# A transformer layer's down projection: written order, and a fourth block by seven half products

## The chip, the core and the metric

The kernel runs on one core of one Trainium2 chip. The metric is the device time of one execution in microseconds (us), the median of repeated runs; lower is better. The engines that appear below are PE (the matrix engine, TensorE), DVE (VectorE, elementwise work on 128 partitions), ACT (ScalarE), POOL (GpSimd) and SP (SyncE, which here issues the transfers that bring the weights from memory). Each engine works through its own list of instructions in order, and waits on semaphores for the others.

## The reference, cut to what matters

One layer of a diffusion transformer on 256 tokens of width 2048, with a 256-token context prefix: adaLN modulation, one combined q/k/v projection, windowed and global attention, an output projection, a residual with LayerNorm, and then the feed-forward half, where the change is:

```python
def modulate(x, shift, scale):
    return x * (1.0 + scale) + shift

def swiglu(u, w_gate, w_up, w_down):
    return (jax.nn.silu(u @ w_gate) * (u @ w_up)) @ w_down

# x: (1, 256, 2048); w_gate, w_up: (2048, 5632); w_down: (5632, 2048); all float32
x = layer_norm(DN_ALPHA * x + g2 * swiglu(modulate(x, sh2, sc2), w_gate[layer], w_up[layer], w_down[layer]),
               ln2_g[layer], ln2_b[layer])
```

## The kernel before, in words

**A product.** Everything is float32, and PE multiplies in a rounded form of it. So each operand is split in two: `hi` is the rounded value (a cast on ACT) and `lo` what the rounding left (a subtraction on DVE). A product of a 128x128 piece of the left operand with a 128x512 piece of a weight is then three matmuls into one accumulation bank: hi by hi, hi by lo, lo by hi (`mm3`, L333 to L335). A weight piece of 512 rows and 512 columns is loaded whole (1 MB, SP's queue, L303) into one of four `raw` buffers, and split in two halves of 128x1024 elements each (L323 cast, L324 subtraction; `split`, L329 and L330, does the same to any operand). There are four `hi` and four `lo` buffers, taken in turn, so that the splits run at most four halves ahead of PE.

**The feed-forward half.** The hidden width of 5632 is cut into 11 blocks, f = 0 to 10, of 512. For each block the gate and up projections (`project`, in four groups g of input features) give two sums; then come the steps of its tail: `turned` (silu, product, squares), `puts` and `gets` (out to memory and back, which transposes), and `places`, which splits the result into `hTh` and `hTl`, the left operands of the down projection. A tail step doesn't stand where it is due in the code: it is put in a list with a count, and each projection call or each step of the down projection counts one (`turn`; a step by seven products counts two at its end). When the count is reached, the tail step's instructions are written down there. ACTIVATE 2, PUT 6, GET 8 and PLACE 9 are the counts.

**The down projection** makes 256 tokens (two tiles t of 128) by 2048 columns, in two pairs of column blocks of 512 (`pair(0)` and `pair(2)`). The sum over the 11 blocks f can be done in two ways. A plain step takes a block f and one column block: one load, two halves of splits, 24 matmuls. A step by seven products takes f and both column blocks of a pair: the 256x512 left operand and the 512x1024 weight are cut into quarters, and Strassen's method in Winograd's form gives the product of the two 2x2 arrangements with seven products of quarters in place of eight. Such a step has two loads, seven splits, 42 matmuls (a pair of plain steps has 48), and four additions or subtractions of weight quarters on DVE, 128x1024 elements each (`by_quarters`). The sums of left quarters that it needs are made once per block (`quarter_sums`, by `QUARTERS`: the count for `places` and that for the sums). The seven products go to three extra banks (p5, p6, p7), and to the banks of the ordinary sums; when all steps by seven products are done, `combine_parts` puts the extra banks into the second column block's sums. `first_block` and `second_block` then apply the gate row (L1245), add to the residual (L1246) and take statistics (L1249) for a column block that is done.

Before the change f = 8, 9 and 10 go by seven products, and a pair is done in the order `ORDER`: first all f for the first column block (with the steps by seven products among them), then the plain f for the second. The gate and up projections stand inside a region whose engines keep the written order. The down projection stands outside it: there a scheduler with costs of its own sets the order on each engine, and only the last column block's end on DVE and ACT is in written order. Of the second pair's last column block the last three plain steps are loaded and split together, and their matmuls are then done tile by tile of tokens, so that token tile 0 is complete while PE works on tile 1; `ending` normalises and stores each. One of the three is split into a `raw` buffer instead of the `hi` and `lo` ones (it is called `hilo` in the rows).

Of the kernel before, what the change touches and what calls it, by code (L numbers as in the profile page):

```python
# [23 lines left out]
P = 128  # L24
# [38 lines left out]
GATE_ROWS = ((17, 20, 23, 23, 24, 27), (43, 44, 47, 47, 48, 51))  # L63
# [195 lines left out]
def dit_layer(ctx: ExitStack, tc: tile.TileContext, x, c, cx, c_ctx, w_ada, b_ada, w_in, q_norm_g,  # L259
# [1266 lines left out]
    u2h = pb.tile([P, KD, SEQ], F32R, tag="u2h", name="u2h")  # L1526
    u2ls = [pb.tile([P, KD // 2, SEQ], F32R, tag=f"u2l{i}", name="u2l") for i in range(2)]

    def u2l(k, n=1):
        half = u2ls[k // (KD // 2)]  # L1530
        k %= KD // 2
        return half[:, k : k + n, :] if n > 1 else half[:, k, :]
# [3 lines left out]
    def z_part(kk):  # L1536
# [9 lines left out]
        nc.scalar.copy(u2h[:, kk : kk + 2, :], uf)  # L1546
        nc.vector.tensor_tensor(u2l(kk, 2), uf, u2h[:, kk : kk + 2, :].bitcast(F32), op=ALU.subtract)
# [11 lines left out]
    def project(accs, w_, f, g, first, last, seeded=False):  # L1559
        w = load_split(w_, g * 4, f * NB)  # L1560
        for j in range(4):
            k = g * 4 + j
            for t in range(NT):
                mm3(accs[t], u2h[:, k, t * P : (t + 1) * P], u2l(k)[:, t * P : (t + 1) * P], w[j],
                    k == first and not seeded, k == last, seeded)
# [27 lines left out]
    quarters, room = {}, {}  # L1593

    def quarter_sums(f, hf):
        i = list(QUARTERS).index(f)
        if i == 0:
            both = pb.tile([P, 2, 2, 4, 2, P], F32R, tag="u2h", name="quarters")
            room["q"] = [both[:, 0], both[:, 1], pb.tile([P, 2, 4, 2, P], F32R, tag="u2l0", name="quarters")]
            room["x"] = pb.tile([P, 2, 2 * NB], F32, tag="u2l1", name="sums")  # L1600
        quarters[f] = [room["q"][i][:, c] for c in range(2)]
        sums = room["x"][:, 0].rearrange("p (s q t) -> p s q t", s=4, q=2)
        s1, s2, s3, s4 = (sums[:, c].rearrange("p q (a i) -> p q a i", a=4) for c in range(4))
        (a11, a12), (a21, a22) = ([hf[t].rearrange("p (a q i) -> p q a i", a=4, q=Q)[:, k : k + 2] for k in (0, 2)]
                                  for t in range(NT))
        for o, x0, x1, op in ((s1, a21, a22, ALU.add), (s2, s1, a11, ALU.subtract), (s3, a11, a21, ALU.subtract),
                              (s4, a12, s2, ALU.subtract)):
            nc.vector.tensor_tensor(o, x0, x1, op=op)
        split(*quarters[f], sums)
# [65 lines left out]
    def z_rest(t, kk):  # L1675
# [7 lines left out]
        nc.scalar.copy(u2h[:, kk : kk + 2, tt], uf)  # L1683
# [121 lines left out]
    def plain(f, n, accs, begins, ends):  # L1805
        w = load_split(w_down, f * 4, n * NB)
        for t in range(NT):
            mms(f, w, t, accs[t], begins, ends)
# [160 lines left out]
```

## Time and profile before

| | |
|---|---|
| median of 3 runs | 1126.13 us (1125.84 to 1126.19) |
| the profiled execution | 1126.5 us, span from first to last instruction 1124.6 us |
| mean granted clock of PE | 0.996 |
| down projection, from the trace | from about 890 us of the span on; the last matmul starts at 1111.01 |

A row of a timeline gives the start in us, the duration, the engine, the line, the operation, what is written and read, and how many instructions the row holds; in square brackets the engine's idle time ahead of it and what ended that. A row of windows gives a stretch, its length, and for each of PE, its weight loads, DVE, ACT and POOL the busy time with the number of instructions that touch the stretch; then PE's granted clock, the busy share of the transfer engines, and GB/s. PE's matmuls overlap: a matmul that is shown with 0.39 us starts 0.23 us after the one ahead of it.

### The profile page before, as it was taken

Reading aid. Unit: us, or ns where it says so; the run is one execution under the profiler, and the core shown is the slowest. Engines: PE = TensorE matmul, PEld = TensorE weight load, DVE = VectorE, ACT = ScalarE, POOL = GpSimd, SP = SyncE. Lnnn points to the kernel's source line nnn. Section 1 sums busy time; section 2 is a strip of 40 time slices with the busy share of each in tenths; the row PEclk is TensorE's granted clock in tenths of the full one; section 3 lists DMA queues with packets and bytes.
Section 4 is the critical chain, followed back from the end, with each engine's and each line's share of the span. In section 5 each row is a group of like instructions: output and inputs, shape, how many; then the busy total and the mean of one; then the engine's idle time right before and its main releaser. Section 6 shows DMA issues by size and latency. Waiting matters only on the chain. (4 is left out here: it accounts for less than half of the span.)

```text
span 1124.6 us, 14148 instructions
## 1 busy us (share of the span) xinstructions
PE 1104.0 (98%) x5241; PEld 893.6 (79%) x5241; DVE 905.8 (81%) x1097; ACT 604.1 (54%) x879; POOL 39.8 (4%) x79
## 2 busy tenths in 40 slices
PE   8999999999999999999999999999999999999995
PEld 7677788788887787888888888888888788888884
DVE  3758999999998998778666876887875899678876
ACT  3335574887684355444564455655554565345541
POOL 1000040101200010000000000000000000000000
PEclk9999999999999999999999999999999999999998
DMA  9999999697999789989858798889896576546651
GB/s 299 388 389 382 386 362 371 227 313 209 358 318 378 267 317 326 341 304 341 287 197 290 266 349 284 302 310 306 302 318 219 169 251 215 194 143 243 226 204 75
DMA packets 179241, 321.26 MB, mean 286 GB/s; under 512 B 8762, under 2 KB 51162, under 8 KB 176867
## 3 DMA queue, kind: packets, MB, share of 16 engines
q1 hardware_dynamic: 177364, 319.25, 80.9%
q10 hardware_dynamic: 1808, 1.11, 0.3%
q8 instruction: 41, 0.67, 0.2%
q14 instruction: 28, 0.23, 0.1%
HBM read 304.07 MB, written 16.25 MB: 285 GB/s over the span
## 5 line engine op out<-in xcount | busy, mean ns | idle before, releaser
L324 DVE TENSOR_TENSOR lo<-raw,hi 128x1024 fp32r<-128x1024 f32 x234 | 282.8, 1221 | 129.0 <-ACT hi L323 126.8
L323 ACT CAST hi<-raw 128x1024 fp32r<-128x1024 f32 x234 | 245.4, 1055 | 247.3 <-PE acc L335 121.7
L334 PE MATMUL acc<-lo,u2h 128*128 128x512 f32 x448 | 175.0, 391 | 0.8 <-DVE lo L324 0.8
L335 PE MATMUL acc<-hi,u2l 128*128 128x512 f32 x448 | 174.6, 390 | 0.1
L333 PE MATMUL acc<-hi,u2h 128*128 128x512 f32 x448 | 174.3, 391 | 0.0
L601 ACT CAST hi<-raw 128x1024 fp32r<-128x1024 f32 (+1 forms) x86 | 87.4, 1030 | 90.5 <-PE acc L335 41.1
L452 DVE SCALAR_TENSOR_TENSOR adav<-raw,cs,adav 128x1024 f32<-128x1024 f32 (+1 forms) x96 | 114.3, 1191 | 6.1 <-DMA raw<-in_w_ada_dram 4.5
L604 DVE TENSOR_TENSOR lo<-raw,hi 128x1024 fp32r<-128x1024 f32 (+1 forms) x86 | 101.4, 1192 | 21.4 <-ACT hi L601 21.4
L333 PE MATMUL acc<-hi,hTh 128*128 128x512 f32 x272 | 105.8, 389 | 0.6 <-ACT hi L329 0.6
L334 PE MATMUL acc<-lo,hTh 128*128 128x512 f32 x272 | 105.8, 389 | 0.0
L335 PE MATMUL acc<-hi,hTl 128*128 128x512 f32 x272 | 105.7, 389 | 0.0
L333 PE MATMUL acc<-hi,uh 128*128 128x512 f32 x256 | 103.5, 404 | 0.1
L335 PE MATMUL acc<-hi,ul 128*128 128x512 f32 x256 | 100.2, 391 | 0.0
L334 PE MATMUL acc<-lo,uh 128*128 128x512 f32 x256 | 99.9, 390 | 0.0
L335 PE MATMUL wk<-hi,u2l 128*128 128x512 f32 x256 | 99.6, 389 | 0.0
L334 PE MATMUL wk<-lo,u2h 128*128 128x512 f32 x256 | 99.6, 389 | 0.0
L334 PEld LDWEIGHTS acc<-lo,u2h 128*128 128x128 f32 x448 | 84.1, 188 | 19.5 <-DVE lo L324 2.2
L333 PE MATMUL wk<-hi,u2h 128*128 128x512 f32 x256 | 99.6, 389 | 0.0
L333 PEld LDWEIGHTS acc<-hi,u2h 128*128 128x128 f32 x448 | 84.1, 188 | 18.7 <-ACT u2h L1683 1.1
L335 PEld LDWEIGHTS acc<-hi,u2l 128*128 128x128 f32 x448 | 84.1, 188 | 17.9 <-DVE u2l L1684 0.7
L333 PEld LDWEIGHTS acc<-hi,uh 128*128 128x128 f32 x256 | 48.2, 188 | 16.0 <-issue 4.6
L333 PEld LDWEIGHTS acc<-hi,hTh 128*128 128x128 f32 x272 | 51.1, 188 | 11.7 <-ACT hi L329 1.0
(287 smaller groups left out, 1742.2 us busy)
## 6 DMA issues: line engine op xcount, KB each, us to landing
raw<-in_w_ada_dram SPq DMA_DIRECT2D x63, 1024.0 KB
raw<-in_w_up_dram SPq DMA_DIRECT2D x44, 1024.0 KB
raw<-in_w_gate_dram SPq DMA_DIRECT2D x44, 1024.0 KB
raw<-in_w_down_dram SPq DMA_DIRECT2D x44, 1024.0 KB
raw<-in_w_ada_dram SPq DMA_DIRECT2D x66, 512.0 KB
raw<-in_w_in_dram SPq DMA_DIRECT2D x18, 1024.0 KB
raw<-in_w_out_dram SPq DMA_DIRECT2D x16, 1024.0 KB
pd<-hx SPq DMA_DIRECT2D x64, 128.0 KB
```

The costliest lines, as they stand in the source:

```text
L323: nc.scalar.copy(hi[:, :n], raw[:, s : s + n])
L324: nc.vector.tensor_tensor(lo[:, :n], raw[:, s : s + n], hi[:, :n].bitcast(F32), op=ALU.subtract)
L333: nc.tensor.matmul(ps, lhsT=xh, rhs=w[0], start=first, stop=False, skip_group_check=seeded)
L334: nc.tensor.matmul(ps, lhsT=xh, rhs=w[1], start=False, stop=False, skip_group_check=seeded)
L335: nc.tensor.matmul(ps, lhsT=xl, rhs=w[0], start=False, stop=last, skip_group_check=seeded)
L452: nc.vector.scalar_tensor_tensor(a[:, c : c + piece], raw[:, f : f + piece], cs[:, 4 * (g * (G4 * NB // w) + j) + 2, None], a[:, c : c + p ...
L601: nc.scalar.copy(hl.hi[:, :n], raw.t[:, s : s + n])
L604: nc.vector.tensor_tensor(hl.lo[:, :n], raw.t[:, s : s + n], hl.hi[:, :n].bitcast(F32), op=ALU.subtract)
```

## The change

Four things are altered together.

1. Block 7 goes by seven products too: four of eleven blocks. The orders of the two pairs are written out (`ORDERS`: `a` is a plain step for the first column block, `b` for the second, `s` a step by seven products).
2. `down()` as a whole stands in the region of written order, on all five engines.
3. The last block's (f = 10) gate and up calls go by feature groups: gate and up of group 0, then of group 1, and so on. The modulated input `u2h`, `u2l` is kept in four-group tiles, and the space of a group that both have read goes to the sums of left quarters, so that those of f = 7 and 8 are made beside block 10's calls, and those of f = 9 and 10 in the down projection's first steps.
4. In a step by seven products the order is b, p1, a, p7, p5, p6, c instead of p1, b, a, p7, p5, p6, c, and the combinations of weight quarters are made in place in the `raw` buffers rather than in two buffers of their own; three of the four stand behind p1's split. The sums of left quarters are split in two halves of 128x512 (with a buffer for two sums) instead of one piece of 128x1024. At the end `first_block` of the second pair is written behind the loads and splits of the last three steps.

```diff
-QUARTERS = {8: (9, 13), 9: (10, 11), 10: (9, 9)}
-ORDER = (0, 1, 8, 2, 3, 9, 4, 5, 6, 10, 7)
+QUARTERS = {7: (9, 13), 8: (10, 11), 9: (10, 9), 10: (9, 9)}
+ORDERS = ("a0 a1 a2 s7 a3 a4 s8 a5 a6 b0 s9 b1 b2 b3 s10 b4 b5 b6", "a0 a1 a2 s7 a3 a4 s8 a5 a6 s9 b0 b1 s10 b2 b3 b4 b5 b6")
...
     def quarter_sums(f, hf):
         i = list(QUARTERS).index(f)
-        sums = room["x"][:, 0].rearrange("p (s q t) -> p s q t", s=4, q=2)
...
-        for o, x0, x1, op in ((s1, a21, a22, ALU.add), (s2, s1, a11, ALU.subtract), (s3, a11, a21, ALU.subtract),
-                              (s4, a12, s2, ALU.subtract)):
-            nc.vector.tensor_tensor(o, x0, x1, op=op)
-        split(*quarters[f], sums)
+        hi, lo = quarters[f] = [pb.tile([P, 4, 2, P], F32R, tag=f"u2{c}{i}", name="quarters") for c in "hl"]
+        pair = pb.tile([P, 2, 2, P], F32, tag="qs", name="sums")
...
+        nc.vector.tensor_tensor(one, a21, a22, op=ALU.add)
+        nc.vector.tensor_tensor(two, one, a11, op=ALU.subtract)
+        split(hi[:, 0:2], lo[:, 0:2], pair)
+        nc.vector.tensor_tensor(one, a11, a21, op=ALU.subtract)
+        nc.vector.tensor_tensor(two, a12, two, op=ALU.subtract)
+        split(hi[:, 2:4], lo[:, 2:4], pair)
...
-    calls = [(f, i, g) for f in gus for i in range(2) for g in range(groups[f], ng)]
+    calls = [(f, i, g) for f in gus if f < SPLIT_F for i in range(2) for g in range(groups[f], ng)]
+    calls += [(f, i, g) for f in range(SPLIT_F, FFN // NB) for g in range(ng) for i in range(2)]
...
         for name, left, right, after in (
-            ("p1", "a11", b11, (x1, b22, b12, sub)),
-            ("b", "s4", b22, (b12, b12, b11, sub)),
-            ("a", "a12", b21, (x2, x1, b11, add)),
-            ("p7", "s3", x1, (b21, b21, x2, sub)),
+            ("b", "s4", b22, None),
+            ("p1", "a11", b11, ((b22, b22, b12, sub), (b12, b12, b11, sub), (b11, b22, b11, add))),
+            ("a", "a12", b21, None),
+            ("p7", "s3", b22, ((b21, b21, b11, sub),)),
             ("p5", "s1", b12, None),
-            ("p6", "s2", x2, None),
+            ("p6", "s2", b11, None),
             ("c", "a22", b21, None),
         ):
...
+    def down():
+        parts, combine_parts, first_block, second_block, _ = pair(0)
+        head, rest = parts("b6")
+        run(head)
+        combine_parts()
+        run(rest)
+        first_block()
+        parts, combine_parts, first_block, last_block, bank = pair(2)
+        head, mid, rest, end = parts("a2", "b1", "b4")
+        run(head)
+        second_block()
+        run(mid)
+        l2_loads()
+        run(rest)
+        combine_parts()
+        ws = [load_split(w_down, f * 4, 3 * NB, spare=f == 6) for f in (4, 5, 6)]
+        first_block()
         for t in range(NT):
-            gated(t, 3, two[5]("bd"[t]), t2k("yt"))
+            for f, w in zip((4, 5, 6), ws):
+                mms(f, w, t, bank("bd"[t]), False, f == 6)
+        for t in range(NT):
+            gated(t, 3, bank("bd"[t]), t2k("yt"))
             spread(t, 3)
             ending(t)
+
+    with tc.manual_schedule(engines={ET.DVE, ET.Activation, ET.PE, ET.Pool, ET.SP}):
+        down()
```

Three places on DVE show what the written order does. The first is the tail of block 10 (`hTl`, then the sums of its left quarters, `sums` and `quarters`) in pair 0, with the splits of the weights around it (`lo`). Before:

```order
L324 TENSOR_TENSOR lo_7927<-raw_7920,hi_7926 128x1024
L330 TENSOR_TENSOR hTl_7955<-hf_7918,hTh_7954 128x4x128
L1608 TENSOR_TENSOR sums_7614<-hf_7918 128x256
L1608 TENSOR_TENSOR sums_7614<-hf_7916,hf_7918 128x256
L1608 TENSOR_TENSOR sums_7614<-sums_7614,hf_7916 128x256
L324 TENSOR_TENSOR lo_7969<-raw_7966,hi_7968 128x1024
L1608 TENSOR_TENSOR sums_7614<-hf_7916,sums_7614 128x256
L324 TENSOR_TENSOR lo_7973<-raw_7966,hi_7972 128x1024
L330 TENSOR_TENSOR quarters_7613<-sums_7614,quarters_7613 128x1024
```

Now, behind the last split of s8 (`lo_7966`) and ahead of the first of a5 (`lo_7999`):

```order
L330 TENSOR_TENSOR lo_7966<-raw_7899,hi_7965 128x1024
L330 TENSOR_TENSOR hTl_7980<-hf_7975,hTh_7979 128x4x128
L330 TENSOR_TENSOR hTl_7980<-hf_7977,hTh_7979 128x4x128
L1604 TENSOR_TENSOR sums_7987<-hf_7977 128x256
L1605 TENSOR_TENSOR sums_7987<-sums_7987,hf_7975 128x256
L330 TENSOR_TENSOR quarters_7986<-sums_7987,quarters_7985 128x512
L1607 TENSOR_TENSOR sums_7987<-hf_7975,hf_7977 128x256
L1608 TENSOR_TENSOR sums_7987<-hf_7975,sums_7987 128x256
L330 TENSOR_TENSOR quarters_7986<-sums_7987,quarters_7985 128x512
L324 TENSOR_TENSOR lo_7999<-raw_7996,hi_7998 128x1024
L324 TENSOR_TENSOR lo_8003<-raw_7996,hi_8002 128x1024
```

Splits of weights stood among the tail's instructions before; now all of the tail stands in one piece ahead of the next split. On ACT the casts of block 10's tail likewise stand in one piece between the casts of s8 and a5.

The second place is a step by seven products in pair 2. Before:

```order
L1832 TENSOR_TENSOR sums_7614<-raw_8670,raw_8668 128x1024
L1832 TENSOR_TENSOR raw_8668<-raw_8668 128x2x512
L330 TENSOR_TENSOR lo_8673<-raw_8668,hi_8672 128x1024
L330 TENSOR_TENSOR lo_8684<-raw_8670,hi_8683 128x1024
L1832 TENSOR_TENSOR sums_7614<-sums_7614,raw_8668 128x1024
L330 TENSOR_TENSOR lo_8695<-raw_8670,hi_8694 128x1024
L1832 TENSOR_TENSOR raw_8670<-raw_8670,sums_7614 128x2x512
L330 TENSOR_TENSOR lo_8706<-sums_7614,hi_8705 128x1024
L330 TENSOR_TENSOR lo_8717<-raw_8668,hi_8716 128x1024
L330 TENSOR_TENSOR lo_8727<-sums_7614,hi_8726 128x1024
L330 TENSOR_TENSOR lo_8737<-raw_8670,hi_8736 128x1024
```

Now:

```order
L330 TENSOR_TENSOR lo_8747<-raw_8744,hi_8746 128x1024
L330 TENSOR_TENSOR lo_8757<-raw_8742,hi_8756 128x1024
L1827 TENSOR_TENSOR raw_8744<-raw_8744,raw_8742 128x2x512
L1827 TENSOR_TENSOR raw_8742<-raw_8742 128x2x512
L1827 TENSOR_TENSOR raw_8742<-raw_8744,raw_8742 128x2x512
L330 TENSOR_TENSOR lo_8770<-raw_8744,hi_8769 128x1024
L330 TENSOR_TENSOR lo_8780<-raw_8744,hi_8779 128x1024
L1827 TENSOR_TENSOR raw_8744<-raw_8744,raw_8742 128x2x512
L330 TENSOR_TENSOR lo_8791<-raw_8742,hi_8790 128x1024
L330 TENSOR_TENSOR lo_8801<-raw_8742,hi_8800 128x1024
L330 TENSOR_TENSOR lo_8811<-raw_8744,hi_8810 128x1024
```

The step has the same eleven instructions. The first load's buffer (`raw_8668` before, `raw_8742` now) was read for the last time by the fifth split, and now is by the sixth.

The third place is the end: the last splits (`lo`, `hilo`), `first_block` of pair 2 and the start of the last column block's end (`yt`). Before, `first_block`'s last rows (L1878 to L1249) stood ahead of the splits of the last five steps:

```order
L1878 TENSOR_TENSOR u_8996<-acc_8440,u_8996 128x512
L1245 TENSOR_TENSOR u_8996<-u_8996,adav_6163 128x512
L1246 TENSOR_TENSOR xt_76<-xt_76,u_8996 128x512
L1249 BN_STATS stats_77<-xt_76 128x6
L324 TENSOR_TENSOR lo_9090<-raw_9087,hi_9089 128x1024
...
L324 TENSOR_TENSOR hilo_9180<-raw_9175,hilo_9180 128x1024
L324 TENSOR_TENSOR lo_9168<-raw_9165,hi_9167 128x1024
L324 TENSOR_TENSOR lo_9172<-raw_9165,hi_9171 128x1024
L1245 TENSOR_TENSOR yt_9257<-acc_8538,adav_6163 128x512
```

Now:

```order
L324 TENSOR_TENSOR lo_9218<-raw_9211,hi_9217 128x1024
L324 TENSOR_TENSOR hilo_9223<-raw_9221,hilo_9223 128x1024
L324 TENSOR_TENSOR hilo_9226<-raw_9221,hilo_9226 128x1024
L1882 TENSOR_TENSOR c1_9189<-acc_8489,c1_9189 128x512
L1245 TENSOR_TENSOR c1_9189<-c1_9189,adav_6168 128x512
L1246 TENSOR_TENSOR xt_76<-xt_76,c1_9189 128x512
L1249 BN_STATS stats_77<-xt_76 128x6
L1882 TENSOR_TENSOR u_9190<-acc_8502,u_9190 128x512
L1245 TENSOR_TENSOR u_9190<-u_9190,adav_6168 128x512
L1246 TENSOR_TENSOR xt_76<-xt_76,u_9190 128x512
L1249 BN_STATS stats_77<-xt_76 128x6
L1245 TENSOR_TENSOR yt_9309<-acc_8599,adav_6168 128x512
```

`first_block` has moved behind the last splits, and the two `hilo` splits behind the last pair of `lo`.

More of the change, by code (lines that the diff above doesn't have):

```diff
@@ L1803, in mms @@
             mm3(ps, hTh[f][:, j, tt], hTl[f][:, j, tt], w[j], first and j == 0, last and j == 3)
[L1805 to L1808, printed above, removed]
-        turn()
     def by_quarters(f, n, bank, begins, ends):
@@ L1851, in begins, with step, plain_step @@
             return fresh
[L1853 to L1862 removed]
+        order = ORDERS[n // 2].split()
+        last = {k: [o for o in order if o[0] == k][-1] for k in "abs"}
+        steps = {}
+        def step(kind, f):
+            if kind == "s":
+                return lambda: by_quarters(f, n, bank, begins, f"s{f}" == last["s"])
+            ps, col = ("ac", n) if kind == "a" else ("bd", n + 1)
+            def plain_step():
+                w = load_split(w_down, f * 4, col * NB)
+                for t in range(NT):
+                    mms(f, w, t, bank(ps[t]), begins(ps[t]), f"{kind}{f}" == last[kind] and kind == "b")
+                turn()
+            return plain_step
+        for o in order:
+            steps[o] = step(o[0], int(o[1:]))
         def combine_parts():
```

95 lines of the change are left out of this document (30 added, 65 removed).

## The prediction

> **What bounds the kernel now.** I read the page's busy times first, then PE's waits in the down projection, then the windows and timelines around the places that the change touches.
>
> ```profile
> PE 1104.0 (98%) x5241; PEld 893.6 (79%) x5241; DVE 905.8 (81%) x1097; ACT 604.1 (54%) x879; POOL 39.8 (4%) x79
> PE acc L333 <- ACT hi L329: 0.6, 1, 0.6
> 1052.76 0.39 PE L333 MATMUL wk<-hi,hTh 128*128 128x512 f32 x1
> 1060.91 0.39 PE L333 MATMUL acc<-hi,hTh 128*128 128x512 f32 x1
> 1111.01 0.39 PE L335 MATMUL acc<-hilo,hTl 128*128 128x512 f32 x1
> ```
>
> PE is busy for 98% of the span, and from 870 us on it shows one wait, of 0.6 us: PE sets the pace of the down projection. What a matmul costs there is read from starts, not durations: a step by seven products begins its first product at 1052.76 and its seventh at 1060.91, with 36 matmuls between, so 8.15 / 36 = 0.226 us each. A product is then 1.36 us, a step by seven products (42) 9.52, a plain step (24) 5.44. Because rows of 0.39 us overlap, a PE that falls behind by a few tenths still looks busy; so a stall is found by counting matmuls:
>
> ```profile
> 890.00:895.00 5.00, 4.96 (x22) 3.78 (x21) 5.00 (x5) 2.77 (x3) 0.00 (x0) 1.00 0.41 113
> 895.00:900.00 5.00, 4.39 (x20) 3.31 (x19) 5.00 (x8) 3.87 (x4) 0.00 (x0) 1.00 0.46 140
> 900.00:905.00 5.00, 4.98 (x23) 3.78 (x22) 5.00 (x6) 3.52 (x6) 0.00 (x0) 1.00 0.94 341
> 905.00:910.00 5.00, 5.00 (x24) 4.14 (x23) 5.00 (x5) 1.87 (x2) 0.00 (x0) 1.00 0.97 346
> ```
>
> Here, where the down projection starts, DVE is busy in all of each 5 us and PE gets 22 + 20 + 23 = 65 matmuls through, against 72 at the rate of the row after: 7 x 0.226 = 1.6 us lost, partly to counting at the edges; I use 1.5. DVE is the second limit, and inside a step by seven products it is near:
>
> ```profile
> 1051.59 1.05 ACT L329 CAST hi<-raw 128x1024 fp32r<-128x1024 f32 x1 [3.02 <-PE acc L335]
> 1052.68 1.23 DVE L330 TENSOR_TENSOR lo<-raw,hi 128x1024 fp32r<-128x1024 f32 x1 [2.74 <-ACT hi L329]
> 1053.94 1.23 DVE L1832 TENSOR_TENSOR raw<-raw,sums 128x1024 f32<-128x1024 f32 x1
> 1055.08 1.22 DVE L330 TENSOR_TENSOR lo<-sums,hi 128x1024 fp32r<-128x1024 f32 x1
> 1056.21 1.22 DVE L330 TENSOR_TENSOR lo<-raw,hi 128x1024 fp32r<-128x1024 f32 x1
> 1057.35 1.22 DVE L330 TENSOR_TENSOR lo<-sums,hi 128x1024 fp32r<-128x1024 f32 x1
> 1058.48 1.22 DVE L330 TENSOR_TENSOR lo<-raw,hi 128x1024 fp32r<-128x1024 f32 x1
> ```
>
> The third product's cast waits 3.02 us for PE to give a buffer back, DVE's split follows, and then DVE runs through the addition, p7, p5, p6 and c without a gap, 1.135 us apart ((1058.48 - 1052.68) / 5 = 1.16 with the first). The step's last split ends at 1059.70, 6.94 after the step's first matmul; it is due at the seventh product, 8.15 after. So DVE is 1.2 us ahead at the end of such a step, and the next split is in time by about as much.
>
> **The change part by part.**
>
> *Fewer matmuls.* One more block by seven products saves 48 - 42 = 6 matmuls in each of two pairs: 12 x 0.226 = **-2.7 us**. Both ends of this are the same; a matmul here has no cheaper form.
>
> *Sums of left quarters beside block 10.* The stall at 890 to 905 is the tails of blocks 8 and 9 with their sums meeting the first splits of the down projection. Those of 7 and 8 now stand among block 10's calls, and those of 9 are taken apart. A plain or projection step needs two splits of DVE's 5.44 us, so about 3.2 us are free in each; the cover is there. I give back the whole stall, **-1.5** (bounds 0, if it only moves, and -1.6).
>
> *Block 10's tail between s8 and a5.* The tail's count of 9 falls on the end of s8 in pair 0, and in written order all of it stands between s8's last split and a5's first. Its pieces:
>
> ```profile
> 920.94 0.68 DVE L330 TENSOR_TENSOR hTl<-hf,hTh 128x512 fp32r<-128x512 f32 x1
> 921.54 0.75 DVE L1608 TENSOR_TENSOR sums<-hf 128x256 f32<-128x256 f32 x2
> 922.21 0.42 DVE L1608 TENSOR_TENSOR sums<-sums,hf 128x256 f32<-128x256 f32 x1
> 902.23 1.13 ACT L329 CAST hTh<-hf 128x512 fp32r<-128x512 f32 x2
> ```
>
> A subtraction of 128x512 takes 0.68 us (0.60 to the next start), a sum of 128x256 0.42, a cast of 128x512 1.13 / 2 = 0.57. Counted from s8's first matmul: the last split of s8 ends at about 7.3 (6.94 before; the three additions in a row ahead of the third product cost 0.3); two hTl to 8.4; two sums to 9.3; cast on ACT to 9.9; subtraction to 10.6; two sums to 11.4; cast to 12.0; subtraction to 12.7. The two sums have one buffer, so the second pair can't be made before the first cast and subtraction are through. ACT's cast for a5 stands behind the last tail cast and ends at 13.0; DVE's split for a5 runs from 13.0 to 14.2. PE needs that split for its second matmul of a5, at 9.52 + 0.23 = 9.75. What is late: 14.2 - 9.75 = **+4.5** (4.2 to 4.8 by this chain; 0 if tail and splits overlapped as before, where the scheduler put splits between the tail's instructions and PE showed no wait). DVE has nothing else to hide it: the ring of four halves lets no split of a5 pass the tail.
>
> *The end.* Before, the last splits, and what follows on DVE:
>
> ```profile
> 1094.84 2.58 DVE L324 TENSOR_TENSOR lo<-raw,hi 128x1024 fp32r<-128x1024 f32 x2 [0.51 <-ACT hi L323]
> 1103.28 0.69 DVE L1245 TENSOR_TENSOR yt<-acc,adav 128x512 f32<-128x512 f32 x1 [5.85 <-PE acc L335]
> 1104.00 0.69 DVE L1246 TENSOR_TENSOR xt<-xt,yt 128x512 f32<-128x512 f32 x1
> 1104.73 0.69 DVE L1249 BATCH_NORM_STATS2 stats<-xt 128x6 f32<-128x512 f32 x1
> 1112.06 0.68 DVE L1245 TENSOR_TENSOR yt<-acc,adav 128x512 f32<-128x512 f32 x1
> ```
>
> DVE was idle for 5.85 us ahead of token tile 0's end (the first yt), and from there to tile 1's yt it works 8.78 us without a gap, although tile 1's last matmul started at 1111.01: from 1103.28 on DVE sets the end. Now two things stand in that idle time: the two hilo splits, which have moved behind the last pair of ring splits (2 x 1.135 = 2.3 us), and the eight instructions of first_block (at the 0.72 us from one dependent 128x512 to the next, 1104.73 - 1104.00, 5.7 us). The last pair ends at 1097.42 as before, since it waits for buffers that PE frees; 1097.4 + 2.3 + 5.7 = 1105.4 against 1103.28: **+2.0** (1.5 to 2.4), and it goes to the end whole. Where first_block stood before, it and the splits had other slack; that gains nothing, since PE did not wait there.
>
> *first_block of pair 0* (written behind b6) and combine_parts (behind b5) put 16 such instructions, 11 us, around two splits of b6, ahead of pair 2's first split. By the same count from b5 this split is in time for a0's matmuls within a few tenths either way: **+0.4** (0 to 0.8).
>
> *The loads.* A step by seven products gives its two raw buffers back late, and the next such step takes them, if two plain steps lie between (two others use the other two buffers). That was so before between steps 8 and 9, and shows in pair 2:
>
> ```profile
> 1009.98 1.22 DVE L330 TENSOR_TENSOR lo<-raw,hi 128x1024 fp32r<-128x1024 f32 x1
> 1011.12 1.22 DVE L330 TENSOR_TENSOR lo<-sums,hi 128x1024 fp32r<-128x1024 f32 x1
> 1012.25 1.22 DVE L330 TENSOR_TENSOR lo<-raw,hi 128x1024 fp32r<-128x1024 f32 x1
> 1011.22 2.64 SPq L303 DMA_DIRECT2D raw<-in_w_down_dram  x2
> 1020.32 1.23 DVE L1832 TENSOR_TENSOR sums<-raw 128x1024 f32<-128x1024 f32 x1 [1.77 <-DMA raw<-in_w_down_dram]
> ```
>
> SP issues the first load when p5's split ends (1011.20) and the second when c's does (1013.47; its issue ends the 2.64 us). The second lands 6.8 us later, at 1020.3, and DVE had waited 1.77 for it. PE, which runs a ring ahead, shows no stall. Now the first buffer is read by p6, so its load goes out one split (1.14 us) later, 1.14 instead of 2.27 ahead of the second. If the second still takes 6.8, it lands 0.3 after it is wanted (c's split at 7.3 instead of 6.94); if it gives back all of the 1.14 that the two loads overlap more, 1.5. Against this stands the slack at p5's split in a step: due at 4 x 1.36 + 0.23 = 5.67, done by 4.67 before (1056.21 + 1.22 - 1052.76, the row above) and by 5.0 with the three additions in a row, so 0.66 us. So a step loses between 0.05 and 0.95; there are four of them (s8 in pair 0; s8, s9 and s10 in pair 2): 0.2 to 3.8, of which I take 0.35 each, nearer the undisturbed row: **+1.4**. If the two loads shared the bandwidth from the start, as nothing here shows, the bound above is 9.8 for the four.
>
> [...]
>
> **Sum.** -2.7 - 1.5 + 4.5 + 2.0 + 0.4 + 1.4 = +4.1 on the profiled execution's 1126.5 (span 1124.6 and 1.9 around it), 1130.6. The median is 0.4 under that execution, so 1130.2. Own range: least, with 4.2, 1.5, 0 and 0.2, +1.7 (1127.8); most, with -1.5 kept as it is, 4.8, 2.4, 0.8 and 3.8, +7.6 (1133.7).
>
> **Rivals.**
>
> *The written order costs nothing.* Tail and splits run as freely as before, first_block finds a place: -2.7 - 1.5, so 1121.9, or with the end's +2.0 alone 1123.9. For it: DVE is busy 81%, ACT 54%, and the profile shows PE hardly waiting. Against it: the tail is one dependent chain between two engines, longer (5.4 us) than the 1.2 us that DVE is ahead, and no slack elsewhere can be borrowed through a ring of four. Chance 0.12.
>
> *The gain and the losses meet.* The chain behind s8 is shorter (say 2 us late, if a5's cast on ACT gets ahead of DVE's tail) and the loads are in time: -2.7 - 1.5 + 2 + 2 + 0.4 = +0.2, 1126.3; up to +2.2. For it: the rows of cast and sum were measured at a busy DVE. Against: ACT's list is in written order too. Chance 0.25.
>
> *Slower still, by loads that share or by PE's clock.* In the four loops, two loads 1.14 apart that share the bandwidth land up to 2.8 us late and cost up to 9.8: 1138.6. This decides from the point at which the second load is more than 0.66 us late. Or the gap behind s8 touches the clock:
>
> ```profile
> 1114.00:1115.00 1.00, 0.00 (x0) 0.00 (x0) 0.90 (x6) 0.00 (x0) 0.00 (x0) 0.89 0.00 0
> 1115.00:1116.00 1.00, 0.00 (x0) 0.00 (x0) 0.93 (x4) 0.32 (x2) 0.00 (x0) 0.50 0.00 0
> ```
>
> After the last matmul (over at 1111.40) the granted clock is 0.50 from about 1114.8, so 3.4 us without matmuls halve it. The gap behind s8 is 13.0 - 9.52 = 3.5 us until a5's first matmul, then one more until 14.2. If the clock drops there and takes 3.4 us to come back, as long as it took to fall, half of that is lost: +1.7, 1131.9, inside my range. [...] Chance of over 1133.7 in all 0.10; that of a clock drop that shows in the granted clock 0.3.
>
> **Chances.** The forecast 0.53, the three rivals 0.12, 0.25 and 0.10. A measurement of this kernel tells about 0.2% from no change, 2.25 us: faster is below 1123.9, slower above 1128.4. The first rival is faster, 0.12; the second the same; the forecast's range lies above 1128.4 but for its lowest 0.6 us, and the third above: 0.63. The range that should hold 8 in 10 goes from the second rival to somewhat over the forecast's upper end, 1126.0 to 1135.5.
>
> **What would show it.** In the profile after: behind the last matmul of s8 in pair 0 (the second step by seven products) a gap of 3 to 5 us on PE released by a5's cast or split, with the hTl and sums rows on DVE just ahead; 22 to 24 matmuls in every 5 us at the down projection's start; DVE busy without a gap from the last ring split through first_block to the first yt, and that yt 2 us behind the last matmul of tile 0; in pair 2 the cast of b late by a few tenths behind a load, and PE waiting in s8 to s10. I am wrong if PE runs through from s8 to a5, or if the loads of pair 2 make PE wait over a microsecond a step.

## The result, and the profile after

The changed kernel takes 1135.41 us (median of 6 runs, 1134.72 to 1138.58) against 1125.99 (6 runs): the ratio is 1.0086, with a 95% interval of 1.0073 to 1.0099. It is slower by 9.4 us, where +4.2 (1130.2) was forecast. The sign was right. The time lies 0.1 us inside the range that was given (1126.0 to 1135.5) and above what the sum allowed at most (1133.7), and the forecast was less than half of the change.

The page's busy times and PE's waits from 820 us of the span on (total, number, longest), in the changed kernel:

```profile
span 1133.8 us, 14174 instructions
PE 1105.6 (98%) x5229; PEld 892.9 (79%) x5229; DVE 927.1 (82%) x1120; ACT 610.5 (54%) x890; POOL 40.8 (4%) x79
PE acc L333 <- ACT hi L323: 3.8, 1, 3.8
PE wk L334 <- DVE lo L330: 0.9, 3, 0.4
PE acc L334 <- DVE lo L324: 0.9, 2, 0.5
PE acc L334 <- DVE lo L330: 0.5, 1, 0.5
```

PE has 12 instructions fewer, as the sum said, and is still "busy 98%": the share tells nothing of the 9 us. Where there was one wait of 0.6 us there are now seven, and one of them is long. I count what a wait costs from one matmul's start to the next, less the 0.227 us that lie between them otherwise.

The start of the down projection, as windows (PE, weight loads, DVE, ACT, POOL with their counts; granted clock):

```profile
890.00:895.00 5.00, 5.00 (x24) 4.14 (x23) 4.80 (x5) 1.93 (x2) 0.00 (x0) 1.00 0.64 214
895.00:900.00 5.00, 5.00 (x23) 4.14 (x23) 5.00 (x5) 3.79 (x4) 0.00 (x0) 1.00 0.00 0
900.00:905.00 5.00, 5.00 (x23) 4.14 (x23) 5.00 (x6) 3.82 (x5) 0.00 (x0) 1.00 0.40 129
```

24 + 23 + 23 matmuls where 22 + 20 + 23 stood: the stall of the tails of blocks 8 and 9 is gone. Counted from start to start, PE lost 1.5 us there before and loses nothing now.

The long wait, behind s8 in pair 0. PE, then DVE and ACT between:

```profile
925.27 0.39 PE L335 MATMUL acc<-hi,hTl 128*128 128x512 f32 x1
929.50 0.80 PE L333 MATMUL acc<-hi,hTh 128*128 128x512 f32 x1 [3.84 <-ACT hi L323]
930.76 0.80 PE L334 MATMUL acc<-lo,hTh 128*128 128x512 f32 x1 [0.47 <-DVE lo L324]
931.36 0.63 PE L335 MATMUL acc<-hi,hTl 128*128 128x512 f32 x1
923.60 1.29 DVE L330 TENSOR_TENSOR hTl<-hf,hTh 128x512 fp32r<-128x512 f32 x2
925.26 0.42 DVE L1605 TENSOR_TENSOR sums<-sums,hf 128x256 f32<-128x256 f32 x1
925.72 0.62 ACT L329 CAST quarters<-sums 128x512 fp32r<-128x512 f32 x1 [3.24 <-DVE sums L1605]
926.37 0.69 DVE L330 TENSOR_TENSOR quarters<-sums,quarters 128x512 fp32r<-128x512 f32 x1 [0.68 <-ACT quarters L329]
927.89 0.62 ACT L329 CAST quarters<-sums 128x512 fp32r<-128x512 f32 x1 [1.55 <-DVE sums L1608]
928.41 3.88 ACT L323 CAST hi<-raw 128x1024 fp32r<-128x1024 f32 x4
928.54 0.69 DVE L330 TENSOR_TENSOR quarters<-sums,quarters 128x512 fp32r<-128x512 f32 x1 [0.68 <-ACT quarters L329]
929.48 4.63 DVE L324 TENSOR_TENSOR lo<-raw,hi 128x1024 fp32r<-128x1024 f32 x4 [0.25 <-ACT hi L323]
```

This is the chain of the forecast, link by link: hTl, two sums, cast, subtraction, two sums, cast, subtraction, and then a5's cast (928.41) and split (929.48). PE loses 4.00 us until a5's first matmul and 1.03 until its second. But the matmuls behind it last 0.80 and 0.63 instead of 0.39, and here is why (the windows of one us; the granted clock is the third number from the end):

```profile
928.00:929.00 1.00, 0.00 (x0) 0.00 (x0) 0.46 (x1) 1.00 (x2) 0.00 (x0) 0.99 0.92 365
929.00:930.00 1.00, 0.50 (x1) 0.29 (x1) 0.75 (x2) 1.00 (x2) 0.00 (x0) 0.50 0.95 389
934.00:935.00 1.00, 1.00 (x4) 0.81 (x3) 0.11 (x1) 0.00 (x0) 0.00 (x0) 0.50 0.92 336
935.00:936.00 1.00, 1.00 (x4) 0.77 (x4) 0.00 (x0) 0.00 (x0) 0.00 (x0) 0.60 1.08 389
```

The clock falls at 928.97 and comes back at 935.80 (0.60 is 0.8 of the window at a half). In that time the matmuls stand 0.43 us apart; it costs another 2.4 us.

A step by seven products in pair 2 (s10), when its second load lands, and what PE waits for:

```profile
1068.62 0.37 SPq L303 DMA_DIRECT2D raw<-in_w_down_dram  x1
1075.78 2.00 ACT L329 CAST hi<-raw 128x1024 fp32r<-128x1024 f32 x2 [4.15 <-DMA raw<-in_w_down_dram]
1086.20 3.49 DVE L330 TENSOR_TENSOR lo<-raw,hi 128x1024 fp32r<-128x1024 f32 x3
1086.73 0.39 PE L333 MATMUL wk<-hi,quarters 128*128 128x512 f32 x1
1087.47 0.50 PE L334 MATMUL wk<-lo,quarters 128*128 128x512 f32 x1 [0.35 <-DVE lo L330]
```

The load takes 7.1 us from its issue, the cast waits for it, and 10.4 us later DVE begins p5's split (1086.20), whose end PE has to wait for. The same happens in s8 of pair 0 (0.46 us lost), s8 (0.40) and s9 (1.44, in two places); here it is 0.62: 2.9 in all.

The end, on DVE:

```profile
1102.31 2.58 DVE L324 TENSOR_TENSOR lo<-raw,hi 128x1024 fp32r<-128x1024 f32 x2 [0.25 <-ACT hi L323]
1104.81 2.35 DVE L324 TENSOR_TENSOR hilo<-raw,hilo 128x1024 fp32r<-128x1024 f32 x2
1107.08 0.68 DVE L1882 TENSOR_TENSOR c<-acc,c 128x512 f32<-128x512 f32 x1
1112.64 0.67 DVE L1245 TENSOR_TENSOR yt<-acc,adav 128x512 f32<-128x512 f32 x1
```

DVE goes from the last ring split through hilo and first_block to the first yt without a gap. From the last matmul's start (1118.47) to the end of the span (1133.8) it is 15.3 us, against 13.6 before (1111.01 to 1124.6): +1.7.

The ledger of the span's +9.2: matmuls -2.7, the start's stall -1.5, the gap behind s8 +5.0, the half clock +2.4, steps by seven products +2.9, first_block at the pairs' border +0.7, the end +1.7. That is +8.5; 0.25 arose before the down projection's first matmul (at 878.48 before, and not at about 890 as the table ahead has it; at 878.73 now), and 0.45 I can't place.

### The profile page after: what moved, and what is told of

Read it like the earlier page. It is cut to its first block, busy times and chain, and to the rows that moved or that the text cites. A ratio compares the mean times of both kernels' runs of the same rounds, so it can differ in the third digit from the quotient of the medians.

```text
span 1133.8 us, 14174 instructions
## 1 busy us (share of the span) xinstructions
PE 1105.6 (98%) x5229; PEld 892.9 (79%) x5229; DVE 927.1 (82%) x1120; ACT 610.5 (54%) x890; POOL 40.8 (4%) x79
## 4 chain that ended last, share of the span: by engine, by line
PE 75%; DVE 13%; DMA 6%; issue 2%; ACT 2%; SPq 1%; DVEq 0%; ACTq 0%; POOL 0%; POOLq 0%
PE acc L333 17%; PE acc L334 17%; PE acc L335 17%; PE wk L334 6%; PE wk L335 6%; PE wk L333 6%; DVE lo L330 4%; DVE raw L1827 3%; DMA raw<-in_w_down_dram 3%; PE wk L1128 2%; DVE csum L716 2%; DMA raw<-in_w_in_dram 2%; SPq L578 1%; PE wk L652 1%; DMA raw<-in_w_ada_dram 1%
## 5 line engine op out<-in xcount | busy, mean ns | idle before, releaser
L324 DVE TENSOR_TENSOR lo<-raw,hi 128x1024 fp32r<-128x1024 f32 x226 | 270.7, 1220 | 105.7 <-ACT hi L323 100.9
L323 ACT CAST hi<-raw 128x1024 fp32r<-128x1024 f32 x226 | 236.2, 1054 | 218.4 <-PE acc L335 110.8
L333 PE MATMUL acc<-hi,hTh 128*128 128x512 f32 x248 | 97.8, 394 | 3.8 <-ACT hi L323 3.8
L334 PE MATMUL acc<-lo,hTh 128*128 128x512 f32 x248 | 98.0, 395 | 1.4 <-DVE lo L324 0.9
L335 PE MATMUL acc<-hi,hTl 128*128 128x512 f32 x248 | 97.6, 393 | 0.0
L329 ACT CAST hi<-raw 128x1024 fp32r<-128x1024 f32 x56 | 58.6, 1054 | 65.0 <-PE acc L335 40.4
L330 DVE TENSOR_TENSOR lo<-raw,hi 128x1024 fp32r<-128x1024 f32 x56 | 66.0, 1220 | 23.6 <-ACT hi L329 23.0
```

The source lines that it names most:

```text
L323: nc.scalar.copy(hi[:, :n], raw[:, s : s + n])
L324: nc.vector.tensor_tensor(lo[:, :n], raw[:, s : s + n], hi[:, :n].bitcast(F32), op=ALU.subtract)
L329: nc.scalar.copy(hi, src)
L330: nc.vector.tensor_tensor(lo, src, hi.bitcast(F32), op=ALU.subtract)
L333: nc.tensor.matmul(ps, lhsT=xh, rhs=w[0], start=first, stop=False, skip_group_check=seeded)
L334: nc.tensor.matmul(ps, lhsT=xh, rhs=w[1], start=False, stop=False, skip_group_check=seeded)
```

## The experiments

All are edits of the changed kernel (1135.41) unless said otherwise; all times are medians, ratios go against the kernel before on the same chip.

**Block 10's tail, spread.**

```diff
-QUARTERS = {7: (9, 13), 8: (10, 11), 9: (10, 9), 10: (9, 9)}
+QUARTERS = {7: (9, 13), 8: (10, 11), 9: (10, 9), 10: (10, 15)}
```

> Block 10's tail in pair 0 moves from behind s8 to behind a5 (places) and behind b1 (sums of left quarters). Theory: PE's gap between s8 and a5 (4.00 + 1.03 us in the changed kernel) is the tail's chain, and the half clock behind it (2.4 us of slower matmuls, granted clock 0.50 from 929 to 936 us) is its consequence; a plain step's slack hides each part. Both go: 1135.4 - 7.4 = 1128.0 us, granted clock 0.996 as before. Rival: in written order the tail's 5.4 us cost the same wherever they stand, only spread: about 1133, with the clock whole (only the 2.4 comes back). Second rival: a5's weights are late, not the tail: 1135.

Measured: 1128.45, ratio 1.0022 (1.0013 to 1.0032), 7.0 us less. The gap and the half clock are gone, the mean clock is 0.995. What is left of the tail is 0.6 us at b2, behind the sums. In written order its place decides what it costs.

**The tail, shorter.** For block 10 the second pair of sums gets a buffer of its own:

```diff
+        pairs = [pair, t2k("sums2").rearrange("p (c q t) -> p c q t", c=2, q=2) if f == 10 else pair]
...
+        if f == 10:
+            split(hi[:, 0:2], lo[:, 0:2], pair)
+        split(hi[:, 2:4], lo[:, 2:4], pairs[1])
```

> The tail stays behind s8, but the second pair of sums of block 10 has a buffer of its own and is made ahead of the first split: four sums, then two casts and two subtractions. The chain is about 1.8 us shorter by the durations, so PE's gap until a5's first matmul is some 2.3 us instead of 3.8. Theory of the clock gate (a gap of over 3.4 us halves the clock, a shorter one doesn't): 1.8 of gap and all of the 2.4 of slow matmuls come back, 1135.4 - 4.2 = 1131.2, and no window of the granted clock near it is under 0.9. Rival: the clock falls after any such gap: 1133.6, with 0.5 in the windows behind s8.

Measured: 1134.34 (1.0075; 1.0060 to 1.0090), 1.1 less; PE's loss until a5's first matmul fell from 4.00 to 2.55, and the clock fell all the same, as the rival has it. A gap need not be 3.4 us long for that; the 3.4 of the expectation is a single interval, at the end of the kernel before (last matmul over at 1111.40, clock at a half from 1114.77). Windows of this kernel:

```profile
925.00:926.00 1.00, 0.72 (x4) 0.26 (x2) 0.97 (x3) 0.18 (x1) 0.00 (x0) 1.00 1.04 403
928.00:929.00 1.00, 0.61 (x1) 0.19 (x1) 0.91 (x1) 1.00 (x3) 0.00 (x0) 0.67 0.99 393
934.00:935.00 1.00, 1.00 (x3) 0.79 (x3) 0.00 (x0) 0.00 (x0) 0.00 (x0) 0.50 1.03 385
935.00:936.00 1.00, 1.00 (x5) 0.80 (x4) 0.00 (x0) 0.00 (x0) 0.00 (x0) 0.91 0.76 195
```

PE's last matmul ends at 925.72 and the next starts at 928.11, only 2.4 us later; the clock falls at 928.34 (0.67 in that window), and is back 6.8 us later, at 935.18 (0.91).

**PE kept at work in the gap.** 14 matmuls more, into a bank that the real work begins afterwards:

```diff
+        if f == 8 and n == 0:
+            for _ in range(14):
+                nc.tensor.matmul(bank("d"), lhsT=lefts["a22"][0][:, 0], rhs=hi[:, 0], start=True, stop=True)
         turn()
         turn()
```

> The changed kernel with 14 extra matmuls behind s8 of pair 0, into a bank that isn't begun yet (their result is overwritten): PE has something to do in the gap, which stays as long as it was, since DVE and ACT set it. Theory: the half clock is answered by PE's idleness alone, so the granted clock stays at 1.00 and the 2.4 us of slow matmuls come back: 1133.0. Rival: the slow matmuls behind the gap have another cause (transfers or DVE's reads at that time) and stay: 1135.4.

Measured: 1133.01 (1.0061; 1.0048 to 1.0075). PE's row with the extra matmuls, the first one of a5, and two windows:

```profile
925.04 3.33 PE L1834 MATMUL acc<-hi,hTh 128*128 128x512 f32 x14
929.08 0.49 PE L333 MATMUL acc<-hi,hTh 128*128 128x512 f32 x1 [0.70 <-ACT hi L323]
929.00:930.00 1.00, 0.49 (x1) 0.19 (x1) 0.94 (x1) 1.00 (x3) 0.00 (x0) 1.00 0.58 238
931.00:932.00 1.00, 1.00 (x6) 0.83 (x5) 1.00 (x2) 0.88 (x1) 0.00 (x0) 1.00 0.00 0
```

a5 still starts 4.0 us late, counted from s8's last matmul (924.82), but the clock stays at 1.00: idle PE is the cause of the slow matmuls, and they cost the 2.4 us that the trace gave.

**The tail in two pieces.** `10: (9, 10)`: places behind s8, sums behind a5.

> Block 10's places stay behind s8, its sums of left quarters move behind a5: the tail is in two pieces of 1.3 and 4.3 us. Theory: each piece costs what is over the slack there, near 0 to 0.8 behind s8 and 1 to 1.5 behind a5, and neither stretch leaves PE mostly idle for a window of 3.4 us, so the clock stays whole: 1135.4 - 5.0 - 2.4 + 1.5 = 1129.5. Rival: any stall of over a microsecond here drops the clock: 1132.

Measured: 1130.28 (1.0037; 1.0025 to 1.0049). PE loses 0.5 us behind s8 and 1.5 behind a5, with the clock at 1.00 throughout. The two stalls together are 2.0 rather than 1.5; the rest is as expected. That PE would have to be mostly idle for 3.4 us was my estimate from that single interval; what this trace shows is a whole clock with 0.96 us without matmuls between 930 and 933.

**p1 ahead of b.**

```diff
-            ("b", "s4", b22, None),
-            ("p1", "a11", b11, ((b22, b22, b12, sub), (b12, b12, b11, sub), (b11, b22, b11, add))),
+            ("p1", "a11", b11, None),
+            ("b", "s4", b22, ((b22, b22, b12, sub), (b12, b12, b11, sub), (b11, b22, b11, add))),
```

> In a step by seven products p1 goes ahead of b again (the three combinations stay in place and follow b's split). Theory: in the steps two plain steps apart PE waits because of a loop: the second load lands (7.1 us after issue), a cast, then nine DVE instructions to p5's split, two more to c's, which frees the buffer for the next load: 21.1 us against PE's 20.4. With p1, which reads the first load, ahead, one DVE instruction less stands behind the second landing: 20.0. The waits of s8 in pair 0 (0.46), of s8, s9, s10 in pair 2 (0.40, 1.44, 0.62) go but for 0.4: 1135.4 - 2.5 = 1132.9. Rival: the loads are late because the first buffer is freed by the sixth split and both loads then overlap; that is as it was: 1135.4.

Measured: 1132.35 (1.0054; 1.0039 to 1.0069), 3.1 less. PE's waits from 860 us on in this kernel:

```profile
PE acc L333 <- ACT hi L323: 3.8, 1, 3.8
PE acc L334 <- DVE lo L324: 1.0, 2, 0.5
```

All three are waits of plain steps, two behind s8 and one at the pairs' border. No step by seven products waits any more, though the first load's buffer is freed as late as before: shortening the chain behind the second landing is enough.

**p7 last.** The first load's buffer free one instruction sooner:

```diff
-            ("p7", "s3", b22, ((b21, b21, b11, sub),)),
             ("p5", "s1", b12, None),
-            ("p6", "s2", b11, None),
+            ("p6", "s2", b11, ((b21, b21, b11, sub),)),
+            ("p7", "s3", b22, None),
```

> In a step by seven products p7 goes behind p5 and p6, so that the first load's buffer is free one DVE instruction sooner (1.14 us), 2.27 ahead of the second as before the change; the loop from the second landing to c's split is as long as in the changed kernel. Theory of the loop: the second load lands 0.3 sooner by less overlap, p5 is due a product sooner but its split too: 0.2 to 0.4 back per step, 1134.0 to 1134.8. Theory of the prediction (the late release of the first buffer makes the second land late): all 2.9 us of the waits in these steps come back, 1132.5.

Measured: 1132.35 (1.0051; 1.0038 to 1.0065). The median is that of the kernel with p1 ahead, and what the prediction's theory gave, but the trace does not bear that theory out: the waits in these steps come down from 2.9 us to 1.6 and don't vanish. In pair 2 they go from 2.5 us to 0.4; in pair 0's s8 they rise from 0.5 to 1.2. The gap behind s8 grows by 0.4 us, and the half clock behind it lasts 3.4 us here and costs 1.6 instead of 2.4. Here PE was back at work 1.05 us before the clock fell (930.05, 931.10), in the changed kernel 0.53 after it (929.50, 928.97).

The second loads of s8, s9 and s10 in pair 2 land 6.7, 6.7 and 5.8 us after issue; in the changed kernel it was 7.0, 7.9 and 7.1. So the late release of the first buffer, which the forecast blamed, is a cause too: it makes the second load land 0.3 to 1.2 us later. From one landing to the next it takes 13.9 us to the end of c's split (1075.78 to 1089.69 in s10 of the changed kernel) and 7.1 for the load, 21.0 against PE's 20.4, and that is the half microsecond a step. The edit with p1 takes a DVE instruction from behind the landing, this one at least 0.3 from the load. But the new order also brings p5 and p6 forward, so how much of the waits the release alone makes is not shown.

**The LayerNorm rows' loads later**, behind `combine_parts` of pair 2.

> The changed kernel with the four loads of the last LayerNorm's rows (2 MB in all) issued behind combine_parts of pair 2, 40 us later. Theory: these loads, issued at 1049.4 to 1051.5, take bandwidth from s9's second load, which lands 7.9 us after issue instead of 7.1, and s9 waits 1.44 us instead of about 0.6: 0.8 us back, 1134.6. Rival: the second load of s9 is late because s8 was, and the rows' loads don't matter: 1135.4.

Measured: 1134.35 (1.0071; 1.0058 to 1.0085), 1.1 less. s9's second load lands 7.5 us after issue instead of 7.9, and its waits come to 1.07 instead of 1.44. This alone doesn't show that the rows' loads slow it: in the kernel with p7 last they come just as soon behind it (2.7 us in both), and it lands after 6.7. And 0.9 of the time arose elsewhere: in this profile the down projection begins at 877.80 instead of 878.73.

**The end's order.** The spare block is split ahead of the last ring splits:

```diff
-        ws = [load_split(w_down, f * 4, 3 * NB, spare=f == 6) for f in (4, 5, 6)]
+        raws = [load_raw(w_down, f * 4, G4, 3 * NB, NB) for f in (4, 5, 6)]
+        w4, w6, w5 = split_raw(raws[0]), split_raw(raws[2], True), split_raw(raws[1])
+        ws = [w4, w5, w6]
```

> At the end the spare (hilo) block is split ahead of the last pair of ring splits, as before the change; first_block stays behind all splits. Theory: DVE's 2.3 us of hilo splits go into the time in which it waits for PE to free ring buffers; first_block is done by the time token tile 0's sums are: the end comes 1.7 us sooner, 1133.7, and the first yt waits for PE, not for DVE. Rival: the tail's 1.7 us come from first_block's eight instructions alone, which still stand there: 1135.4 to 1135.0.

Measured: 1134.18 (1.0073; 1.0058 to 1.0089), 1.2 less. DVE at the end:

```profile
1105.60 0.68 DVE L1882 TENSOR_TENSOR c<-acc,c 128x512 f32<-128x512 f32 x1
1110.54 0.69 DVE L1249 BATCH_NORM_STATS2 stats<-xt 128x6 f32<-128x512 f32 x1
1111.15 0.67 DVE L1245 TENSOR_TENSOR yt<-acc,adav 128x512 f32<-128x512 f32 x1
```

first_block starts 12.3 us ahead of the last matmul (1117.91) where it was 11.4, and from the last matmul to the end it is 14.4 us instead of 15.3: 0.9 back. But DVE still goes into the first yt without a gap; that it would wait for PE there, as I had expected, was wrong. It works without a gap from `combine_parts` on, which stands right ahead of these splits (1093.16 in this kernel).

**All of it together.** Block 10's counts are (10, 16), p1 goes ahead of b, the end is in that order, and `combine_parts` is cut in two halves with a plain step between, in both pairs.

> The changed kernel with block 10's places behind a5 and its sums behind b2 in pair 0; p1 ahead of b; the spare block's splits ahead of the last ring splits; and combine_parts in two halves, one step apart, in both pairs, so that first_block of pair 0 and the end of pair 2 find DVE free sooner. If the waits found are all there is, what stays is 12 matmuls less (-2.7) and the stall at the start of the down projection that the changed kernel doesn't have (-1.5): 1126.0 - 4.2 = 1121.8, and no PE wait over 0.3 us behind 860 us. Rival: the written order keeps some DVE work in the way at the end or at the pairs' border: 1123 to 1124.5.

Measured: 1123.84 (10 runs), ratio 0.9978 (0.9968 to 0.9987): faster than the kernel before by 0.2%. PE's waits from 860 us on:

```profile
PE acc L334 <- DVE lo L324: 0.6, 1, 0.6
```

That is the pairs' border, which cutting `combine_parts` did not help (0.8 lost); DVE is also still 1 us late for the first yt. These account for most of the 2 us by which it misses 1121.8, and are what the rival named. With p7 last in addition:

> The best version so far with p7 behind p5 and p6 as well. Theory: the two waits of 0.33 us left in pair 2 (one of them in s8) were DVE's chain in a step; the one in s8 goes, 1123.5. Rival: nothing left there that p7's place decides: 1123.8 or a little over.

Measured: 1123.51, ratio 0.9980 (0.9971 to 0.9989), not told apart from the one before. The 0.33 us in s8 are gone, the border's wait is 1.0.

**The fourth block alone.** The kernel of "all together" with block 7 in plain steps, `QUARTERS = {8: (10, 11), 9: (10, 9), 10: (10, 15)}`, and the orders written for that.

> The best version so far (1123.84) with block 7 taken back to plain steps: three blocks of eleven by seven products, everything else as it is there. Theory of the prediction's first term: 12 matmuls more, 2.7 us, less 0.3 for one step less that waits: 1126.2 to 1126.6. Rival: with DVE that near its limit a fourth block is worth less than its matmuls, since its additions and splits delay others: 1124 to 1125.

Measured: 1133.10 (1.0057; 1.0045 to 1.0070), far off both. A wait that I had built in myself; SP's rows in this kernel, ACT's, PE's around the gap, and a window:

```profile
1056.31 0.80 SPq L1793 DMA_DIRECT2D l<-in_ln_b_dram  x2
1057.21 2.33 SPq L303 DMA_DIRECT2D raw<-in_w_down_dram  x4
1064.83 1.99 ACT L323 CAST hi<-raw 128x1024 fp32r<-128x1024 f32 x2 [8.59 <-DMA raw<-in_w_down_dram]
1062.92 0.39 PE L335 MATMUL acc<-hi,hTl 128*128 128x512 f32 x1
1065.92 0.79 PE L333 MATMUL acc<-hi,hTh 128*128 128x512 f32 x1 [2.62 <-ACT hi L323]
1065.00:1066.00 1.00, 0.07 (x1) 0.08 (x1) 0.10 (x1) 1.00 (x2) 0.00 (x0) 0.71 0.95 352
```

The LayerNorm rows go to the rooms of the first two blocks' sums of left quarters. With three blocks these are 8 and 9, s9 still reads them, and on SP the weight loads wait in line behind: four come out at once at 1057.21, and PE loses 3.8 us and then the half clock (0.71 is 0.58 of that window at a half, so from 1065.42). With the rows' loads moved behind `combine_parts`:

> The kernel with three blocks again, now with the loads of the last LayerNorm's rows behind combine_parts of pair 2: in the run before, these loads waited on SP for s9 to be done with their rooms (with three blocks these hold the sums of left quarters of blocks 8 and 9), and the weight loads queued behind them came late (PE's gap of 2.8 + 1.0 us at 1063 and the half clock after it). Theory: without that the fourth block's worth shows, 2.7 us over the best version's 1123.5 to 1123.8: 1126.2 to 1126.5. Rival: less, 1124 to 1125.5, as DVE is relieved by three blocks too.

Measured: 1126.71, ratio 1.0006 (0.9997 to 1.0015); 2.9 us over the version with four blocks (1123.84; the rows' loads stand earlier there). Leaving out waits (1.5 us in each), the down projection's matmuls take 231.1 us here and 228.4 there: 2.7, as 12 x 0.226 gives. So the first term of the sum is real. Three blocks in this arrangement are no faster than the kernel before.

## Why the prediction was right or wrong

*Fewer matmuls, -2.7:* right; three blocks against four measured 2.9 in time, 2.7 on PE.

*The stall at the start, -1.5:* right. PE lost 1.5 us there before and loses nothing now.

*Block 10's tail, +4.5:* the mechanism, the place and the order of the links were right; the gap measured 5.0. From the end of s8's last split (921.33 + 2.35, 923.6 with the overlap) to the end of a5's (930.7) it takes 7.1 us where I had 6.9, as the casts last 0.62; the other 0.3 is s8's own: its last split ends 1.7 us before its last matmul starts (925.27), so at 7.6 by the forecast's count and not 7.3. That is not its second load's doing: with p1 ahead s8 doesn't wait, and its last split ends 1.7 us before its last matmul all the same. What makes it 0.3 later I haven't found. (The handovers between the engines are 0.03 to 0.04 us in the rows of that chain: 925.68 to 925.72, 926.34 to 926.37.)

*The clock:* this is the step that failed. The sum has no term for it: the half clock stood as a rival, with a chance of 0.3 and a price of 1.7, because the gap of 3.5 us lay at the edge of 3.4, which was one interval of the kernel before, and "takes 3.4 us to come back" was a guess (6.8 in the changed kernel). It cost 2.4, the largest part of what the sum missed. The gap halved the clock in all six profiles that have the whole tail behind s8 and nothing else for PE in the gap, in one (the tail, shorter) even with a gap of 2.4; the half clock lasted 6.8 us (once 3.4, with p7 last). A gap that is priced at over two us of nearly idle PE should have carried this in the sum. The clock fell 2.1 us (three blocks) to 5.3 us (p7 last) after the last matmul; in the shorter gap 1.0 us of matmuls stood in the 3.4 us ahead of its fall.

*The loads, +1.4:* right in kind, too small by half: 2.9. I expected b's cast late behind a load, but had not counted what stands behind that landing: a cast of 1.05 us, where before DVE began with a combination at the landing itself (1020.32 in the prediction's rows). From there nine DVE instructions lead to the end of p5's split, before and now; the experiment with p1 takes one of them out, and the waits are gone. The late release, which the term was built on, makes the second load land 0.3 to 1.2 us later; I had taken a value near the lower end, 0.35, where only s8 lies (0.3). Why s9's load came latest (7.9) is open. The term's arithmetic was off too: lateness of 0.3 to 1.5 less 0.66 of slack gives 0 to 0.84 a step, not 0.05 to 0.95; and 2.8 us late, which I had estimated and no run shows, would cost 8.6 in four steps, not 9.8.

*The border, +0.4:* 0.7, inside its bounds. *The end, +2.0:* 1.7.

Of +5.2 that the sum missed, 2.4 are the clock, 1.5 the loads, 0.5 the chain, 0.3 the border; the end takes 0.3 off, and the rest was lost before the down projection or isn't placed. That 1135.4 still lies in the range, by 0.1, is luck: the upper end was put somewhat over the sum's most, 1133.7, without a term for it.

The rivals that the written order costs little are out: the gap, the clock and the steps' waits vanished when an order was altered by hand, with the same work in the kernel. The third rival was half right: the clock fell, but the second of two loads close together landed 0.3 to 1.2 us later and not 2.8.

## What to carry to other kernels

With DVE and ACT over half busy, the order that a scheduler found can hide a short chain in the gaps of others; written out by hand, the same chain becomes a wait where it stands in one piece (7.4 us behind s8), and costs 0.6 us where it is spread over plain steps. Price a loop (load, splits, release of its buffer) as a whole against PE's period, since a few tenths over it return in every turn. And add to each gap of PE of two us or more what a halved clock costs behind it (2.4 us here, 1.6 to 2.8 in seven profiles), or keep PE at work meanwhile.

## What the hardware showed that I had not expected

The granted clock fell after PE had been idle for as little as 2.1 us (in the kernel with three blocks, at 1065.42, with the last matmul over at 1063.31). It stayed at 1.00 with 1.5 us without matmuls between 928 and 931 (PE kept at work in the gap: 0.38, 0.49 and 0.66 us of them in the three windows) and with 0.96 between 930 and 933 (the tail in two pieces: 0.80, 0.36, 0.88). In seven profiles it fell with work left for PE; it stayed at a half for 6.8 us in six of them and for 3.4 in one (p7 last). The loss behind a gap was 1.6 us in that one and 2.1 to 2.8 in the six, and does not follow the gap's length: the 2.8 stands behind the shortest gap, 2.4 us (the tail, shorter). 14 useless matmuls in the gap saved 2.4 us.

Part of what it does follow can be read from the changed kernel. Its clock changes at 928.97, 935.80 and 1123.53, which lie 6.83 and 187.73 us apart: 2 and 55 times 3.413. Stretches of that length, counted from these changes (PE's time with matmuls is the first number behind the length, the granted clock the third from the end):

```profile
925.56:928.97 3.41, 0.10 (x1) 0.00 (x0) 2.01 (x5) 1.70 (x3) 0.00 (x0) 1.00 0.97 294
928.97:932.39 3.42, 2.42 (x5) 1.63 (x6) 3.17 (x4) 3.32 (x4) 0.00 (x0) 0.50 0.43 176
932.39:935.80 3.41, 3.41 (x10) 2.64 (x9) 1.72 (x2) 0.00 (x0) 0.00 (x0) 0.50 0.75 231
1116.71:1120.12 3.41, 2.15 (x10) 1.46 (x8) 3.41 (x7) 1.13 (x5) 0.00 (x0) 1.00 0.00 0
```

The clock fell at the end of a stretch with 0.10 us of matmuls and not of one with 2.15; at a half, it stayed there at the end of one with 2.42 and came back at the end of one with 3.41. The kernel with p7 last, whose clock is at a half from 931.10 to 934.52, in the same way:

```profile
924.28:927.69 3.41, 1.51 (x7) 0.94 (x5) 2.66 (x6) 0.62 (x1) 0.00 (x0) 1.00 1.03 390
927.69:931.10 3.41, 0.50 (x1) 0.19 (x1) 2.47 (x4) 2.66 (x4) 0.00 (x0) 1.00 0.36 148
931.10:934.52 3.42, 3.21 (x8) 2.53 (x9) 3.42 (x4) 1.74 (x2) 0.00 (x0) 0.50 0.20 42
```

PE ends at 925.79 and is at work again from 930.05, but the clock falls only at 931.10, and is back one stretch later; at 927.69, behind 1.51 us of matmuls, it didn't fall. In the kernel with three blocks it fell with 1.3 us of them in the 3.41 ahead (until 1063.31, then none until 1065.42). So a gap's length alone doesn't decide: in p7 last PE's gap, 4.3 us, is longer than the 3.8 of the changed kernel, and the half clock behind it is half as long. How often a gap of a given length halves the clock, and whether these amounts hold for other kernels, isn't shown.
